# Hybrid S5 and RG-LRU layer: a scratch tensor laid out by channel and stored from ACT's queue, and loads moved from SP's queue to GpSimd's

## The chip, the core and the metric

The kernel runs on one core of one Trainium2 chip. A core has a matrix engine (TensorE, PE in the views; its weight load is PEld), a vector engine (VectorE, DVE), an activation engine (ScalarE, ACT), a general one (GpSimd, POOL), a sequencer for transfers (SyncE, SP) and 16 DMA engines. Each engine takes its own instructions in order and waits on semaphores for the others. SP, ACT and POOL can each issue DMAs; an issue is an instruction in that engine's order. The metric is the device time of one execution in microseconds.

## The reference

One layer over 2048 latent tokens (a 32 by 64 grid) behind 256 context tokens, model width 1024, all in float32. A projection of the normed input gives four parts of 1024 channels each: the S5 input, its gate, the RG-LRU input, its gate. Two recurrences run in both directions, and an output projection joins them:

```python
z = (rmsnorm(h, norm_g[layer]) * (1.0 + sc[:, None]) + sh[:, None]) @ w_in[layer]
u_s5, g_s5, u_lru, g_lru = jnp.split(z, cuts, axis=-1)
y_s5, _ = s5_branch(u_s5, *s5p, init=fin_s5, need_out=True)
y_lru, _ = rglru_branch(to_col_major(u_lru, rows), *lrup, init=fin_lru, need_out=True)
y_lru = to_row_major(y_lru, rows)
h_next = h + gt[:, None] * mix_out(y_s5, g_s5, y_lru, g_lru, w_out[layer])
```

The S5 branch is a complex diagonal recurrence in 64 groups of 16 channels. The RG-LRU branch is a short convolution, two sigmoid gates per direction from 64 by 64 block matrices (16 heads), and a gated scan. `mix_out` multiplies each result by the SiLU of its gate and projects 2048 channels to 1024.

## The kernel before

Every large product is made of three matmuls on numbers split into a high and a low part (`mm3`, lines 248 to 250). The weights of the input projection come in tiles of 128 columns, 512 KB each: `wload` (line 231) loads one into `wraw`, of which there are two, and ACT and DVE split it (lines 240 and 241). The projection runs in two halves of 1024 tokens, half 0 with the context; half 1 reloads the split weights as `w` from a DRAM scratch, WS (line 267).

The S5 input goes through a DRAM scratch, ZU. Before, ZU is laid out by half, step, channel in the group, group and chunk: `[2, T, 8, G, NCH]`. For each block of 128 channels ACT copies the context's part into a tile `zsc` (line 328) and the latent part, in two copies, into a tile `zst` (line 334). `zst` has a single buffer. SP stores each tile in two DMAs (lines 330 and 349), of 64 KB for zsc and 256 KB for zst. While half 0 does this, PE, DVE and ACT also build the S5 tables (W, Wt, psw, kk, lines 630 to 700).

The RG-LRU stage works on eight blocks of 128 channels, two heads each; "head b" below is block b. Its convolution result goes to the scratch XC (POOL's queue, line 383). For head b the loads are `gw` (gate weights, line 402), `xs` (the block with its two heads swapped, two DMAs of 576 KB, line 410) and `xc` (the block, 1152 KB, line 415), all with one buffer and all on SP's queue. `gates` multiplies (line 427) and takes the sigmoids (line 431); then follow tanh, exp and square root on ACT; `finish` runs the scans on DVE (lines 438 to 453) one head later, loads the output gate GL into the dead tile of rr (line 449, POOL's queue) and stores the result to the scratch YL (line 455, POOL's queue). `rr` has three buffers and `gi` four. In this stage PE's order is the one in the code, with the second half's projections between the gates; on all other engines, and in all other stages, a scheduler orders the instructions by priorities and modelled times.

After it the S5 stages run: `s5_inputs` reads ZU as `u` (two groups to a load, line 762), multiplies it by `wt`, and DVE scans the states chunk by chunk (lines 774 to 778); `s5_outputs` reads `u` again and multiplies by `mt` and `et`. As filler beside them `out_lru` multiplies y_lru by the output weights: it loads YL in 16 tiles with `wload` (SP's queue) and stores sums to the scratch HP (POOL's queue, line 864). The gated S5 result and the last product close the kernel.

Of the kernel before, what the change touches and what calls it, by code (L numbers as in the profile page):

```python
# [17 lines left out]
D = 1024  # L18
# [5 lines left out]
G = 64  # L24
NCH = 144
T = 16
# [20 lines left out]
class Block:  # L47
# [180 lines left out]
        return load  # L228


    def wload(self, src):

        raw = self.wp.tile([P, KT, P], F32, tag="wraw", bufs=2, name="wraw")
        self.nc.sync.dma_start(out=raw, in_=src)
        return raw

    def wsplit(self, raw, copy):
# [14 lines left out]
    def projections(self, half, kinds):  # L252

        nc = self.nc
# [38 lines left out]
        raw, nxt = self.first if half == 0 else (load(0), None)  # L293
        w = split(raw, 0)
        raw = nxt or load(1)
        for i, (kind, b, tiles) in enumerate(blocks):
            whi, wlo = w[:, 0], w[:, 1]
            r = slice(b * P, (b + 1) * P)
            if kind == "u_lru" and tiles[0] != 1:
                u = self.conv_input(half, b)  # L300
            if kind == "u_s5":
                st = self.stp.tile([P, T, 64], F32, tag="st4", bufs=1, name="zst")
            for tl in tiles:
                n = 256 if tl == "c" else 512
                xh, xl = self.xh[tl]
                ps = self.psM.tile([P, 512], F32, tag="mm", name="pp")
                for k in range(KT):
                    self.mm3(ps[:, :n], lambda k: whi[:, k, :], lambda k: wlo[:, k, :],
                             lambda k: xh[:, k, :n], lambda k: xl[:, k, :n], (k,))
                    if k < KT - 1:  # L310
                        yield
                if kind == "u_lru":
                    pos = 1 if tl == "c" else (3 if half else LC + 4) + tl % 2 * 512
                    nc.scalar.copy(out=u[:, pos:pos + n], in_=ps[:, :n])
                    if tl == "c":
                        self.conv(half, b, u, 0)
                elif kind == "g_lru":
                    o = self.stp.tile([P, 512], F32, tag="st2", bufs=2, name="ust")
                    if half:
                        nc.scalar.activation(out=o, in_=ps, func=AF.Sigmoid)  # L320
                        nc.vector.tensor_mul(out=o, in0=ps, in1=o)
                    else:
                        nc.scalar.activation(out=o, in_=ps, func=AF.Silu)
                    nc.scalar.dma_start(out=self.GL[r, tl * 512:tl * 512 + 512], in_=o)
                elif kind == "u_s5":
                    if tl == "c":
                        sc = self.stp.tile([P, T, 16], F32, tag="st2", bufs=2, name="zsc")
                        nc.scalar.copy(out=sc[:, ::-1, :], in_=ps[:, :256].rearrange("p (c j) -> p j c", j=T))
                        for kt in range(2):
                            nc.sync.dma_start(out=self.ZU[kt, :, :, b * 8:b * 8 + 8, 0:16].rearrange("h j g c -> g (h j) c"),  # L330
                                          in_=sc[:, kt * 8:kt * 8 + 8, :])
                    else:
                        o = (tl % 2) * 32
                        nc.scalar.copy(out=st[:, ::-1, o:o + 32], in_=ps.rearrange("p (j r) -> p j r", j=T))
                else:
                    o = self.stp.tile([P, 512], F32, tag="st2", bufs=2, name="gst")
                    nc.scalar.activation(out=o.rearrange("p (j a r) -> p a j r", j=8, a=2),
                                         in_=ps.rearrange("p (a j r) -> p a j r", a=2, j=8), func=AF.Silu)
                    nc.scalar.dma_start(out=self.GS[tl, r].rearrange("d j c -> d (j c)"), in_=o)
                if tl == tiles[0] and i + 1 < len(blocks):  # L340
                    w = split(raw, i + 1)
                    raw = load(i + 2)
                yield
            if kind == "u_lru" and tiles[-1] == both[-1]:
                self.conv(half, b, u)
            if kind == "u_s5":
                cs = slice(80, NCH) if half else slice(16, 80)
                for kt in range(2):
                    nc.sync.dma_start(out=self.ZU[kt, :, :, b * 8:b * 8 + 8, cs].rearrange("h j g c -> g (h j) c"),
                                      in_=st[:, kt * 8:kt * 8 + 8, :])  # L350


    def conv_input(self, half, b):
# [33 lines left out]
    def lru(self, lp, le):  # L387

        nc, v = self.nc, self.nc.vector
# [3 lines left out]
        rows = lambda b: slice(b * P, (b + 1) * P)  # L393
        big = lambda tag, n, pool=lp: pool.tile([P, N], F32, tag=tag, bufs=n, name=tag)

        def weights(b):

            gw = le.tile([P, 2, 2, 64], F32, tag="gw", bufs=1, name="gw")
            for w, name in enumerate(("lru_w_a", "lru_w_x")):
                for e in range(2):  # L400
                    src = self.io[name][0, :, 2 * b + e].rearrange("d i j -> i d j")
                    nc.sync.dma_start(out=gw[w * 64:w * 64 + 64, :, e, :], in_=src)
            return gw

        def load_xs(b):

            xs = big("xs", 1, le)
            for e in range(2):
                o = b * P + 64 - e * 64
                nc.sync.dma_start(out=xs[e * 64:e * 64 + 64, :], in_=self.XC[o:o + 64, :])  # L410
            return xs

        def load_xc(b):
            xc = big("xc", 1, le)
            nc.sync.dma_start(out=xc, in_=self.XC[rows(b), :])
            return xc

        def gates(b, d, gw, xcs, rr, gi):
# [39 lines left out]
        gw = weights(0)  # L458
        xs, xc = load_xs(0), load_xc(0)
        yield 4  # L460
        prev = iter(())
        for b in range(8):
# [9 lines left out]
            if b < 7:  # L472
                xs, gw, xc = load_xs(b + 1), weights(b + 1), load_xc(b + 1)
# [283 lines left out]
    def load_u(self, gp, g):  # L757

        u = gp.tile([P, 2, 2, NCH], F32, tag="u", bufs=3, name="u")
        for kt in range(2):  # L760
            src = self.ZU[kt, :, :, g:g + 2].rearrange("h j g c -> (h j) (g c)")
            self.nc.sync.dma_start(out=u[:, kt].rearrange("p g c -> p (g c)"), in_=src)
        return u

    def s5_scan(self, sp, zt, hb):
# [84 lines left out]
    def out_lru(self, wl, hr):  # L850

        nc = self.nc

        def load(j):
            src = self.YL.rearrange("(b p) t -> p b t", p=P)[:, :, j * P:(j + 1) * P]
            raw = self.wload(src)
            if j % 2:
                ht = self.stp.tile([P, T, 64], F32, tag="st4", bufs=1, name="hr1").rearrange("p a b -> p (a b)")
            else:
                ht = hr.tile([P, D], F32, tag="hr", bufs=1, name="hr0")  # L860
            return raw, ht
# [183 lines left out]
    def build(self):  # L1045
        tc, nc = self.tc, self.nc
        with ExitStack() as es:
# [4 lines left out]
            self.XC = dt("XC", [D, LC + L])  # L1052
            self.GL = dt("GL", [D, L])
            self.YL = dt("YL", [D, L])
            self.ZU = dt("ZU", [2, T, 8, G, NCH])
            self.GS = dt("GS", [4, D, T, 32])
            self.YT = dt("YT", [G, T, 8, 2, P])
            self.ZD = dt("ZD", [D, 8, 2, P])
# [165 lines left out]
```

## Time and profile before

| what | value |
|---|---|
| median of three runs | 1836.4 us (1836.33 to 1843.17) |
| profiled execution | 1834.38 us |
| its span | 1832.6 us |
| mean granted clock of PE | 0.969 |
| busy: PE, DVE, ACT, POOL | 1703.5, 1127.4, 864.0, 135.7 us |

The profile is of one execution. The rows further down come from six views. The *page* lists the busiest groups: line, engine, operation, output and inputs, count, then busy time and mean ns, then idle time ahead of them. The *chain* on the page follows the end of the program back to what released each step. A *windows* row is a stretch: its limits and length, busy time (and instructions) of PE, PEld, DVE, ACT and POOL, then the granted clock as a share of full speed, the mean busy share of the 16 DMA engines, and GB/s. A *waits* row names the engine and what it was about to do, what it waited for, the sum, the times and the longest. A *timeline* row is start, duration, engine (SPq is SP's issuing), line, operation, and in brackets the idle time before it and its releaser. A *tile* row gives min/median/max of a duration.

### The profile page before, as it was taken

The numbers are of one execution on the slowest core, as the hardware profiler recorded it, in microseconds if no ns is written. First come the engines' busy times: TensorE is split into PE (matmuls) and PEld (weight loads), VectorE is DVE, ScalarE is ACT, GpSimd is POOL, SyncE is SP. The second block draws the span as 40 slices with busy tenths as digits, with TensorE's granted clock in tenths as the row PEclk, the third lists the DMA queues.
The fourth block names the chain that finished last, engine by engine and source line by source line (L and its number), as shares of the span: only waits on it lengthen the run. The fifth ranks groups of instructions, "written<-read, shape, count | busy, mean of one in ns | idle before, by whom it ended". The sixth has DMA issues, their size and how long they took to land.

```text
span 1832.6 us, 26083 instructions
## 1 busy us (share of the span) xinstructions
PE 1703.5 (93%) x9785; PEld 1378.7 (75%) x9785; DVE 1127.4 (62%) x2006; ACT 864.0 (47%) x1376; POOL 135.7 (7%) x276
## 2 busy tenths in 40 slices
PE   7787899999998997989999899899999999999998
PEld 2666678888877664555567788778898899998886
DVE  5787788777354475679768049898600156336663
ACT  2622222222365386778675798525565443222221
POOL 1021111111110000000000000000000000001111
PEclk9898899999999998989999899999999999999999
DMA  8696577577654754566774988628898657557563
GB/s 258 157 219 182 170 209 230 190 258 270 223 182 151 242 155 165 172 209 206 202 203 133 293 280 263 200 90 263 268 284 263 194 169 211 144 156 219 187 195 89
DMA packets 315631, 373.56 MB, mean 204 GB/s; under 512 B 124669, under 2 KB 258417, under 8 KB 303218
## 3 DMA queue, kind: packets, MB, share of 16 engines
q1 hardware_dynamic: 267312, 235.04, 45.4%
q0 software_dynamic: 21824, 103.30, 15.1%
q10 hardware_dynamic: 26370, 33.57, 5.4%
q8 instruction: 77, 1.26, 0.3%
q14 instruction: 48, 0.39, 0.1%
HBM read 233.49 MB, written 138.35 MB: 203 GB/s over the span
## 4 chain that ended last, share of the span: by engine, by line
PE 55%; DMA 14%; DVE 12%; issue 9%; ACT 7%; SPq 2%; POOL 1%; ACTq 0%; DVEq 0%; POOLq 0%
PE pp L248 6%; PE pp L249 6%; PE pp L250 6%; PE po L250 5%; PE po L248 5%; PE po L249 5%; DMA ZU<-zst 4%; PE pgl L250 3%; PE pgl L248 3%; PE pgl L249 3%; PE py L811 2%; PE py L809 2%; DMA rr<-GL 2%; PE pg L427 2%; DVE p L774 2%
## 5 line engine op out<-in xcount | busy, mean ns | idle before, releaser
L248 PE MATMUL pp<-x,w 128*128 128x512 f32 x1024 | 420.4, 411 | 14.2 <-DMA w<-WS 12.3
L250 PE MATMUL pp<-x,w 128*128 128x512 f32 x1024 | 409.3, 400 | 4.7 <-DVE w L241 4.7
L249 PE MATMUL pp<-x,w 128*128 128x512 f32 x1024 | 409.4, 400 | 0.0
L248 PEld LDWEIGHTS pp<-x,w 128*128 128x128 f32 x1024 | 195.9, 191 | 91.0 <-issue 48.6
L250 PEld LDWEIGHTS pp<-x,w 128*128 128x128 f32 x1024 | 196.1, 191 | 48.9 <-DVE w L241 6.0
L249 PEld LDWEIGHTS pp<-x,w 128*128 128x128 f32 x1024 | 196.5, 192 | 39.9 <-issue 1.3
L241 DVE TENSOR_TENSOR w<-wraw,w 128x1024 fp32r<-128x1024 f32 x66 | 80.5, 1221 | 157.1 <-ACT w L240 143.2
L240 ACT CAST w<-wraw 128x1024 fp32r<-128x1024 f32 x66 | 69.4, 1051 | 159.8 <-PE pp L250 95.3
L381 DVE SCALAR_TENSOR_TENSOR xcv<-uc,vcol,xcv 128x256 f32<-128x256 f32 (+2 forms) x72 | 73.2, 1016 | 56.3 <-ACT xcv L378 54.5
L248 PE MATMUL po<-x,w 128*128 128x512 f32 x256 | 104.1, 407 | 0.8 <-ACT x L841 0.8
L249 PE MATMUL po<-x,w 128*128 128x512 f32 x256 | 100.7, 393 | 0.7 <-DVE x L842 0.7
L250 PE MATMUL po<-x,w 128*128 128x512 f32 x256 | 100.5, 392 | 0.0
L427 PE MATMUL pg<-xs,gw 64*64 64x512 f32 (+1 forms) x320 | 90.8, 594 | 10.3 <-ACT gi L431 10.3
L248 PE MATMUL po<-ws,yh 128*128 128x512 f32 x256 | 99.6, 389 | 0.0
L249 PE MATMUL po<-ws,yh 128*128 128x512 f32 x256 | 99.6, 389 | 0.0
L250 PE MATMUL po<-ws,yl 128*128 128x512 f32 x256 | 99.6, 389 | 0.0
L427 PE MATMUL pg<-xc,gw 64*64 64x512 f32 (+1 forms) x320 | 91.3, 594 | 8.1 <-ACT rr L431 5.3
L746 PE MATMUL pw<-u,wt 128*128 128x144 f32 x512 | 77.2, 300 | 13.3 <-DMA wt<-WD 10.3
L746 PEld LDWEIGHTS pw<-u,wt 128*128 128x128 f32 x512 | 73.0, 201 | 21.2 <-ACT z L753 11.5
L811 PE MATMUL py<-h,et 128*128 128x128 f32 x512 | 79.8, 280 | 9.8 <-ACT h L804 9.6
L774 DVE TENSOR_TENSOR p<-z,A 128x128 f32<-128x128 f32 x288 | 79.9, 291 | 6.3
L809 PE MATMUL py<-u,mt 128*128 128x128 f32 x512 | 79.4, 278 | 0.0
(259 smaller groups left out, 3518.9 us busy)
## 6 DMA issues: line engine op xcount, KB each, us to landing
wraw<-in_w_in_dram SPq DMA_DIRECT2D x50, 512.0 KB
WS<-w POOLq DMA_DIRECT2D x24, 1024.0 KB, 7.3
w<-WS SPq DMA_DIRECT2D x24, 1024.0 KB
u<-ZU SPq DMA_DIRECT2D x128, 144.0 KB
ED<-E POOLq DMA_DIRECT2D x16, 1024.0 KB, 6.1
WD<-Wt POOLq DMA_DIRECT2D x32, 512.0 KB, 5.1
wt<-WD SPq DMA_DIRECT2D x32, 512.0 KB
et<-ED SPq DMA_DIRECT2D x32, 512.0 KB
```

Source lines behind the costliest of these rows:

```text
L240: copy(out=w[:, 0], in_=raw)
L241: self.nc.vector.tensor_sub(out=w[:, 1], in0=raw, in1=w[:, 0])
L248: nc.tensor.matmul(ps, lhsT=whi(k), rhs=xhi(k), start=(k == 0), stop=False)
L249: nc.tensor.matmul(ps, lhsT=whi(k), rhs=xlo(k), start=False, stop=False)
L250: nc.tensor.matmul(ps, lhsT=wlo(k), rhs=xhi(k), start=False, stop=(k == KT - 1))
L381: nc.vector.scalar_tensor_tensor(out=xc, in0=u[:, o + k:o + k + N], scalar=cw[:, k * 8 + b:k * 8 + b + 1], in1=xc, op0=ALU.mult, op1=ALU.add)
L427: nc.tensor.matmul(pss[w][e * 64:e * 64 + 64, :n], lhsT=gw[ws, d, e, :], rhs=xcs[(w + e) % 2][ws, o:o + n], start=True, stop=True, tile_po ...
L746: nc.tensor.matmul(pw[:, c, :], lhsT=w[:, gi, kt, c, :], rhs=u[:, kt, :], start=(kt == 0), stop=(kt == 1))
L774: v.tensor_mul(out=p, in0=cur.unsqueeze(1).to_broadcast([P, 2, 2, 32]), in1=self.A16[:, :, :, gs])
L809: nc.tensor.matmul(o, lhsT=ms(m[:, i * 8:i * 8 + T]), rhs=u[:, i, 16:], start=(i == 0), stop=False)
L811: nc.tensor.matmul(o, lhsT=ms(e[:, i, gi]), rhs=h[:, i, :], start=False, stop=(i == 1))
```

## The change

Three things. ZU is laid out by half, channel, step in the group's eight and chunk, `[2, D, 8, NCH]`; its stores are issued by ACT, and the loads of `u` read two pieces of 576 bytes per partition where they read one of 1152. The loads gw, xs and xc are issued by POOL. The y_lru tiles of `out_lru` are loaded by POOL's queue, for which `wload` takes an engine.

```diff
-    def wload(self, src):
+    def wload(self, src, eng=None):
 
         raw = self.wp.tile([P, KT, P], F32, tag="wraw", bufs=2, name="wraw")
-        self.nc.sync.dma_start(out=raw, in_=src)
+        (eng or self.nc.sync).dma_start(out=raw, in_=src)
...
                         for kt in range(2):
-                            nc.sync.dma_start(out=self.ZU[kt, :, :, b * 8:b * 8 + 8, 0:16].rearrange("h j g c -> g (h j) c"),
-                                          in_=sc[:, kt * 8:kt * 8 + 8, :])
+                            nc.scalar.dma_start(out=self.ZU[kt, r, :, 0:16], in_=sc[:, kt * 8:kt * 8 + 8, :])
...
                 for kt in range(2):
-                    nc.sync.dma_start(out=self.ZU[kt, :, :, b * 8:b * 8 + 8, cs].rearrange("h j g c -> g (h j) c"),
-                                      in_=st[:, kt * 8:kt * 8 + 8, :])
+                    nc.scalar.dma_start(out=self.ZU[kt, r, :, cs], in_=st[:, kt * 8:kt * 8 + 8, :])
...
                     src = self.io[name][0, :, 2 * b + e].rearrange("d i j -> i d j")
-                    nc.sync.dma_start(out=gw[w * 64:w * 64 + 64, :, e, :], in_=src)
+                    nc.gpsimd.dma_start(out=gw[w * 64:w * 64 + 64, :, e, :], in_=src)
...
                 o = b * P + 64 - e * 64
-                nc.sync.dma_start(out=xs[e * 64:e * 64 + 64, :], in_=self.XC[o:o + 64, :])
+                nc.gpsimd.dma_start(out=xs[e * 64:e * 64 + 64, :], in_=self.XC[o:o + 64, :])
...
             xc = big("xc", 1, le)
-            nc.sync.dma_start(out=xc, in_=self.XC[rows(b), :])
+            nc.gpsimd.dma_start(out=xc, in_=self.XC[rows(b), :])
...
         for kt in range(2):
-            src = self.ZU[kt, :, :, g:g + 2].rearrange("h j g c -> (h j) (g c)")
-            self.nc.sync.dma_start(out=u[:, kt].rearrange("p g c -> p (g c)"), in_=src)
+            src = self.ZU[kt, g * 16:(g + 2) * 16].rearrange("(g h) j c -> (h j) g c", g=2)
+            self.nc.sync.dma_start(out=u[:, kt], in_=src)
...
             src = self.YL.rearrange("(b p) t -> p b t", p=P)[:, :, j * P:(j + 1) * P]
-            raw = self.wload(src)
+            raw = self.wload(src, nc.gpsimd)
...
-            self.ZU = dt("ZU", [2, T, 8, G, NCH])
+            self.ZU = dt("ZU", [2, D, 8, NCH])
```

The order of PE's instructions is the same but for one group that moves one place. On ACT the stores of ZU enter. This is ACT in half 0, at blocks 1 and 2 of the S5 input (L334 and L333 copy into zst, L328 into zsc), before:

```order
L334 COPY zst<-pp 128x16x32
L328 COPY zsc<-pp 128x16x16
L686 COPY kk<-psk 128x240
L687 COPY kk<-psk 128x240
L334 COPY zst<-pp 128x16x32
L240 CAST w<-wraw 128x1024
L665 COPY Wt<-psw 128x512 x2
L334 COPY zst<-pp 128x16x32
L328 COPY zsc<-pp 128x16x16
```

and now:

```order
L333 COPY zst<-pp 128x16x32
L348 DMA ZU<-zst 1024x1x64 x2
L328 COPY zsc<-pp 128x16x16
L684 COPY kk<-psk 128x240
L330 DMA ZU<-zsc 1024x1x16 x2
L685 COPY kk<-psk 128x240
L333 COPY zst<-pp 128x16x32
L240 CAST w<-wraw 128x1024
L663 COPY Wt<-psw 128x512 x2
L333 COPY zst<-pp 128x16x32
L348 DMA ZU<-zst 1024x1x64 x2
```

The issues now stand between the copies of the block and those of the tables.

On SP, in the RG-LRU stage at head 5 and the start of half 1's S5 input, the loads of w stood between the loads of xs, gw and xc and the stores of zst:

```order
L410 DMA xs<-XC 64x2304
L267 DMA w<-WS 128x2048
L410 DMA xs<-XC 64x2304
L402 DMA gw<-in_lru_w_a_dram 64x2x64 x2
L402 DMA gw<-in_lru_w_x_dram 64x2x64 x2
L415 DMA xc<-XC 128x2304
L267 DMA w<-WS 128x2048
L1179 DMA gt<-GT 128x1024
L267 DMA w<-WS 128x2048
L349 DMA ZU<-zst 8x128x64 x2
```

Now SP goes from one load of w to the next, and on to the weights of the last projection and the loads of u:

```order
L267 DMA w<-WS 128x2048 x14
L1177 DMA gt<-GT 128x1024
L267 DMA w<-WS 128x2048 x6
L234 DMA wraw<-in_w_in_dram 128x8x128 x6
L760 DMA u<-ZU 128x2x144 x2
L739 DMA wt<-WD 128x1024
```

Nothing is left on SP in this stage that waits for anything but a buffer of w.

On POOL the order there, from head 2's GL to the XC store of block 7, was before:

```order
L449 DMA rr<-GL 128x2048
L455 DMA YL<-gi 128x2048
L383 DMA XC<-xcv 128x1026
L363 MEMSET uc 128x2
L449 DMA rr<-GL 128x2048
L455 DMA YL<-gi 128x2048
L383 DMA XC<-xcv 128x1026
```

and is now, from head 3's GL to the first loads of head 6:

```order
L447 DMA rr<-GL 128x2048
L453 DMA YL<-gi 128x2048
L408 DMA xs<-XC 64x2304 x2
L400 DMA gw<-in_lru_w_a_dram 64x2x64 x2
L400 DMA gw<-in_lru_w_x_dram 64x2x64 x2
L413 DMA xc<-XC 128x2304
L381 DMA XC<-xcv 128x1026
L447 DMA rr<-GL 128x2048
L453 DMA YL<-gi 128x2048
L408 DMA xs<-XC 64x2304 x2
```

The loads of head 5 come behind GL and YL of head 3, those of head 6 behind head 4's, those of head 7 behind head 5's. The loads of heads 3 and 4 stand between GL and YL of heads 1 and 2.

## Rows read from the trace of the kernel before

**Rows 1.** The page: the chain by engine, and the costliest group of matmuls.
```profile
PE 55%; DMA 14%; DVE 12%; issue 9%; ACT 7%; SPq 2%; POOL 1%; ACTq 0%; DVEq 0%; POOLq 0%
...
L248 PE MATMUL pp<-x,w 128*128 128x512 f32 x1024 | 420.4, 411 | 14.2 <-DMA w<-WS 12.3
```

**Rows 2.** Windows by stage (columns as told above), and the first 25 us.
```profile
125.00:225.00 100.00, 78.46 (x455) 61.70 (x454) 74.04 (x95) 19.85 (x38) 16.81 (x27) 0.86 0.61 171
225.00:500.00 275.00, 273.22 (x1663) 221.24 (x1662) 197.65 (x258) 80.02 (x142) 46.84 (x92) 1.00 0.70 230
...
625.00:1000.00 375.00, 341.06 (x1680) 221.80 (x1679) 267.70 (x131) 268.80 (x299) 11.85 (x26) 0.96 0.58 177
...
1078.00:1228.00 150.00, 141.28 (x723) 120.11 (x721) 138.62 (x594) 88.48 (x182) 2.67 (x5) 0.98 0.61 198
1228.00:1650.00 422.00, 413.94 (x3051) 392.34 (x3052) 186.76 (x503) 189.34 (x307) 5.86 (x11) 0.99 0.71 215
...
125.00:150.00 25.00, 21.04 (x111) 17.20 (x117) 23.76 (x31) 4.54 (x8) 7.04 (x8) 0.93 0.62 164
```

**Rows 3.** Waits of ACT and of SP's queue.
```profile
ACT zst L334 <- DMA ZU<-zst: 100.7, 12, 16.3
...
SPq L410 <- PE pg L427: 118.0, 7, 34.5
SPq L415 <- DVE gi L471: 46.7, 5, 17.5
```

**Rows 4.** Timeline of ACT, half 0: a copy into zst.
```profile
158.96 0.59 ACT L334 COPY zst<-pp 128x512 f32<-128x512 f32 x1 [11.66 <-DMA ZU<-zst]
```

**Rows 5.** Timeline of PE behind that copy.
```profile
160.73 1.11 PE L662 MATMUL psw<-ident,W 128*128 128x128 f32 x4 [4.87 <-DVE W L632]
...
162.06 0.63 PE L249 MATMUL pp<-x,w 128*128 128x512 f32 x1
```

**Rows 6.** Windows of shorter stretches.
```profile
125.00:127.00 2.00, 2.00 (x10) 1.62 (x9) 2.00 (x2) 0.00 (x0) 0.53 (x1) 1.00 0.41 68
700.00:725.00 25.00, 13.12 (x61) 8.52 (x61) 11.42 (x8) 24.76 (x23) 0.38 (x2) 0.79 0.53 208
775.00:800.00 25.00, 20.20 (x87) 9.30 (x84) 23.28 (x11) 13.88 (x21) 1.56 (x4) 0.80 0.42 134
846.50:858.50 12.00, 11.14 (x49) 8.71 (x47) 11.86 (x8) 9.93 (x9) 1.07 (x2) 1.00 1.00 343
861.00:985.00 124.00, 116.88 (x591) 76.43 (x589) 91.32 (x39) 90.67 (x100) 3.23 (x6) 0.99 0.65 181
1020.00:1078.00 58.00, 53.75 (x335) 47.53 (x334) 2.45 (x2) 54.02 (x129) 0.00 (x0) 0.96 0.91 290
```

**Rows 7.** The tile ZU: issue times of its stores, min/median/max in ns.
```profile
L349 SPq DMA_DIRECT2D ZU<-zst x32: 583/1206/7050, 124.1 to 983.5; - x32
L330 SPq DMA_DIRECT2D ZU<-zsc x16: 1078/4944/8694, 108.8 to 270.4; - x16
```

**Rows 8.** The chain of waits from 683 to 770 us: start, length, what.
```profile
684.48 11.44 DMA rr<-GL
...
744.61 12.03 DMA rr<-GL
```

**Rows 9.** DMA issues: KB each and median us to landing.
```profile
rr<-GL POOLq DMA_DIRECT2D x8, 1024.0 KB, 7.5
YL<-gi POOLq DMA_DIRECT2D x8, 1024.0 KB, 4.8
```

**Rows 10.** Timeline of ACT behind the first of those loads.
```profile
699.53 0.19 ACT L364 COPY uc<-halo 128x3 f32<-128x3 f32 x1 [15.16 <-DVE xcv L381]
```

**Rows 11.** Timelines of POOL, SP and PE before the gates of head 5.
```profile
846.54 0.53 POOL L455 DMA_DIRECT2D YL<-gi  x1 [10.08 <-DVE gi L453]
...
848.75 0.33 SPq L415 DMA_DIRECT2D xc<-XC  x1
...
858.60 0.43 PE L427 MATMUL pg<-xc,gw 64*64 64x256 f32 x1
```

## The prediction

> **What bounds the kernel now.** I read the chain that ended last first: more than half of it is PE, and the three other large shares, DMA, DVE and ACT, are places where PE waits or runs behind somebody [rows 1]. The table by stages then says where PE has room [rows 2]. It is full in the stretch from 225 to 500 us (273.22 of 275) and nearly so from 1228 to 1650 (413.94 of 422), so nothing that a transfer does there can show. It has room in two stretches that the change touches. From 125 to 225 us, where half 0 of the S5 input is projected, PE works 78.46 of 100 us at a granted clock of 0.86; from 625 to 1000, the RG-LRU stage, 341.06 of 375. From 1078 to 1228 PE has room too, but DVE is busy for 138.62 of the 150 us with the serial scan of the two S5 states: whatever a transfer saves there goes to DVE's next step.
>
> The list of waits names who holds the first stretch up: ACT waited 100.7 us, 12 times, before the copy into zst, for the stores of the zst before [rows 3]. zst has one buffer, so the copy of block b cannot start until both stores of block b-1 have landed. One of them is in the timeline of ACT, 11.66 us before 158.96 [rows 4]. ACT takes its instructions in order, so the copies of kk and Wt behind that zst wait too, DVE's W behind them, and PE: 4.87 us of idle before 160.73, and after it matmuls of 0.63 us [rows 5], against the 0.411 us of the page's mean for line 248 [rows 1]. The clock thus takes a second toll: where PE had been idle the granted level is 1.2 of 2.4 GHz for some microseconds.
>
> Why the stores are slow is in the windows: while almost nothing but pieces of ZU moves, the DMA engines' share stays at 0.41, although with other traffic it reaches 1.00 [rows 6]. I read this as a store that is dealt to half of the 16 engines: its outer dimension is 8 (8x128x64 in the order of SP). SP pays for it as well. An issue for zst takes 1206 ns at the median and up to 7050, one for zsc 4944 and up to 8694 [rows 7], and the weight loads stand behind them.
>
> In the RG-LRU stage the chain of waits shows rr<-GL twice with 11.44 and 12.03 us from issue to landing [rows 8], against a median of 7.5 [rows 9]. The xs loads were issued at the same moment on another queue and moved with it. After the first of these ACT had been idle for 15.16 us [rows 10], and then had so much to catch up that PE worked only 13.12 us between 700 and 725; 775 to 800 has 20.20 at a clock of 0.80 [rows 6]. SP itself stood 118.0 us before xs and 46.7 before xc [rows 3], with the loads of w behind them.
>
> **The change part by part.**
>
> *ZU's layout and its queue, half 0.* The same 1024 pieces per store go to an outer dimension of 1024, so I expect all 16 engines, and landing in about half the time. An ACT wait of 11.66 us ends with a landing that came that much too late [rows 4]; the stores of a block were then under way for more than 12 us. In half the time they land some 6 us sooner or more, and the issues no longer stand behind SP's other ones: I take the wait as gone, or 3 us long at most. The room in this stretch is 100 - 78.46 = 21.5 us of idle PE, and I estimate 4 us for the clock: after each of three such gaps some 4 us of matmuls run at 0.63 instead of 0.411 us, a third of that lost. 25.5 in all. Not all of it comes back. In the first 25 us DVE is busy for 23.76 and PE idle for 4 [rows 2]: that is DVE's own limit, and stays. And ACT now issues: four issues to a block, each at least the 583 ns of the fastest zst issue and, at the median, 1206 [rows 7], so 2.3 to 4.8 us a block in which ACT can't copy. ACT is busy for only 19.85 of the 100 us, so I charge one microsecond of each block, 4.5 in all. 25.5 - 4 - 4.5 = **17 us**. The bounds: 0, if the issues on ACT stretch as they did on SP, and 25.
>
> *ZU in half 1.* From 861 to 985 PE is busy for 116.88 of 124 us [rows 6]: at most 7 us, against 16 issues that enter an ACT with much to do (268.80 of 375 in the stage). Taken as plus 3 and minus 3: nothing.
>
> *xs, xc and gw on POOL's queue.* What it takes away is SP's standing (118.0 and 46.7 us): the w loads behind go out when their buffer is free. What it does to the path is that xs now stands behind rr<-GL on one queue, so GL need not share the engines with it. GL lands in 11.44 and 12.03 us now and should take 6 to 7.5: 4 to 6 us earlier twice, less at the other heads. The idle PE of the stage is 375 - 341.06 = 34 us; 11.9 of it lies in 700 to 725, 4.8 in 775 to 800, where the clock costs more. I take **12 us**: twice 5, and 2 of clock. Bounds: 25 (all but a quarter of the idle time), and the loss priced below. POOL pays some 56 issues of about 0.55 us (that of 846.54 is 0.53) and is busy for 11.85 of the 375 us: nothing by itself; its order is another matter.
>
> *The y_lru loads on POOL's queue.* Sixteen issues leave SP, where they stood before loads of the S5 outputs. From 1078 to 1228 DVE sets the pace, and behind it PE idles only 8 us in 422 [rows 2]: I take 2 us, between 0 and 4. They share POOL's order with the stores of HP, which ACT's copies wait for only through a single buffer; DVE's scan hides that.
>
> *u loads with two pieces per partition.* 128 loads have pieces of 576 instead of 1152 bytes. Between 1020 and 1078 the engines' share is 0.91, but ACT is busy there for 54.02 of 58 us [rows 6], so ACT hides most of it. I charge 1 us, between 0 and 4.
>
> The sum is made on the profiled execution: 1834.4 - 17 - 12 - 2 + 1 = 1804.4. Its time is 2 us below the median of the three runs, 1836.4; I predict **1804**.
>
> **The rivals.**
>
> *ACT pays for the issues.* On SP the ZU issues stretched to 5 and 8 us since the queue was full. If they stretch alike on ACT, the copies of Wt and kk stand behind them as they stood behind the wait: 17 goes to about 0, and in half 1 some of the 12 is eaten. 1834 - 2 + 1, between 1826 and 1838. For it: the pieces stay as small and as many, and the row on SP doesn't show whether they or the load of SP's queue made the issues long. Against it: the fastest zst issue had the same pieces and took 583 ns [rows 7], so the pieces alone don't make it long, and the engines that take them double.
>
> *Only the first stretch gains.* In the RG-LRU stage DMA engines are at 1.00 from 846.5 to 858.5 with 343 GB/s [rows 6]: where bytes are the limit another queue brings nothing, and ACT and PE have nearly equal work. Then 12 goes: 1834.4 - 17 + 1 - 2 = 1816.
>
> The Trainium skill has a rule against the change on the same page, section "Issuing engines are not separate DMA queues": transfers from any issuing engine run on the same 16 DMA engines, and another issuer saves only the sequencer's time. By it the xs, xc, gw and y_lru moves are worth only SP's standing; the row of 343 GB/s agrees for that stretch. It is this rival, 1816.
>
> *POOL's order makes it slower.* In the new order xs, gw and xc of head 5 stand behind YL of head 3, on a queue that is served in order. YL was issued at 846.54, xc of head 5 at 848.75, the gates of that head began at 858.60 [rows 11]. Now YL, xs and xc, 1024 + 1152 + 1152 = 3328 KB, must pass in the 12 us from 846.54. At 343 GB/s they need 10 and are just in time. At the pace of a lone rr<-GL, 1024 KB in 7.5 us [rows 9], they need 24, and the gates start 12 us late. Three heads have this order (5, 6, 7): 36 us, and the 12 us are not won: 1834.4 - 17 - 2 + 1 + 36 = 1852. It decides from the point where POOL's queue moves less than about 280 GB/s. For it: the median of YL is 1024 KB in 4.8 us [rows 9], 213 GB/s. Against it: one transfer alone pays its own latency, and queued ones overlap.
>
> *The gain is larger.* The idle time of both stretches goes almost wholly, 25 + 25 us: 1785 or a little below.
>
> **How the numbers follow.** Forecast, 1793 to 1812: 0.42. Only the first stretch, 1812 to 1825: 0.21. Larger gain, 1776 to 1793: 0.11. ACT pays, 1826 to 1838: 0.13. POOL's order, above 1840: 0.13. I take half a per cent, 9 us, as what a measurement of this kernel tells from no change: faster means below about 1826. Faster 0.42 + 0.21 + 0.11 = 0.74; same 0.13; slower 0.13. The range from 1782 to 1838 leaves out POOL's order and a third of the larger gain, 0.17 in all. The likeliest case's own range is 1793 to 1812.
>
> **What would show each step.** ZU right: ACT's wait before zst nearly gone from the list of waits, PE busy above 90% there, the clock near 1.0, the stage done some 17 us earlier; issues for ZU near 0.6 us on ACT's queue. If they are 3 us and more, ACT paid. GL right: rr<-GL on the chain with 5 to 8 us and no ACT idle of 15 us before the second head. POOL's order: the gates' matmuls (line 427 now) wait for xs or xc, or POOL idles long before YL with xs behind it. SP's list must have lost the waits before xs and xc either way. Wrong altogether would be a stage from 1078 on that moves by more than 5 us: then the y_lru or the u loads do what I priced at nothing.

## The result

| kernel | median of its runs | against before |
|---|---|---|
| before | 1837.8 us (4 runs) | 1 |
| changed | 1816.3 us (1811.1 to 1820.2, 4 runs) | 0.9876 [0.9843, 0.9909] |
| changed, in a later series | 1816.0 us (6 runs; before 1832.9) | 0.9899 [0.9876, 0.9923] |

The change makes the kernel faster by 1.0 to 1.2 per cent, some 17 to 21 us; the prediction said 1804, with 1782 to 1838 as its range. 1816 lies outside the likeliest case's own range, 1793 to 1812, and in that of the rival "Only the first stretch gains", 1812 to 1825, and the gain is short of the 30 us that were forecast. The span of the profiled execution fell from 1832.6 to 1813.2 us.

The page of the changed kernel, busy time by engine: PE is busy for 5 us less with the same instructions, which I put down to the clock; POOL has 72 more instructions, the moved issues.

```profile
PE 1698.5 (94%) x9785; PEld 1372.1 (76%) x9785; DVE 1128.0 (62%) x2006; ACT 864.2 (48%) x1376; POOL 181.8 (10%) x348
```

PE runs the same 9785 instructions in both kernels, in the same order but for one group. So a stretch of one trace can be matched to the stretch of the other that holds the same instructions. The windows of the changed kernel that answer to 125 to 225, to 600 to 625, to 625 to 1000 and to 1228 to 1650 us of before are these (columns: limits, length, busy and count of PE, PEld, DVE, ACT, POOL, clock, DMA share, GB/s); the counts of PE, 455, 110, 1680 and 3051, show the match:

```profile
126.30:203.70 77.40, 71.02 (x455) 55.05 (x454) 71.47 (x93) 20.51 (x39) 16.14 (x26) 1.00 0.71 216
577.70:612.30 34.60, 27.51 (x110) 21.86 (x109) 12.98 (x13) 3.72 (x6) 2.24 (x5) 0.90 0.78 244
612.30:979.30 367.00, 338.48 (x1680) 221.86 (x1679) 268.45 (x131) 268.39 (x299) 39.56 (x75) 0.96 0.57 179
...
1207.30:1630.70 423.40, 414.61 (x3051) 392.72 (x3052) 185.53 (x493) 188.32 (x305) 12.41 (x18) 0.99 0.72 214
```

and the second of them in the kernel before:

```profile
600.20:625.20 25.00, 25.00 (x110) 20.31 (x109) 12.63 (x12) 3.82 (x6) 0.65 (x2) 1.00 1.00 319
```

Against [rows 2] the first stretch went from 100 to 77.4 us, PE's idle time from 21.5 to 6.4 and the clock from 0.86 to 1.00: 22.6 us won. The second went from 25 to 34.6: 9.6 us lost, in a place that the prediction did not look at. The RG-LRU stage went from 375 to 367: 8 won. From 1228 on 1.4 were lost. Together that is -22.6 + 9.6 - 8 + 1.4 = -19.6, and the spans differ by 19.4. So the total is what one of the rivals said, 1816, though not for its reason.

The wait for the stores shrank, though it did not go. From the waits of the whole changed kernel, to be held against [rows 3]:

```profile
ACT zst L333 <- DMA ZU<-zst: 30.7, 6, 10.6
```

The tile ZU, issue times in ns, min/median/max, against [rows 7]:

```profile
L348 ACTq DMA_DIRECT2D ZU<-zst x32: 520/521/1687, 120.3 to 962.2; - x32
L330 ACTq DMA_DIRECT2D ZU<-zsc x16: 520/1265/4033, 102.6 to 236.6; - x16
```

And from ACT's timeline the longest issue of this stretch with the wait behind it, and the other wait that is left there:

```profile
146.27 4.65 ACTq L330 DMA_DIRECT2D ZU<-zsc  x2
153.60 0.59 ACT L333 COPY zst<-pp 128x512 f32<-128x512 f32 x1 [7.37 <-DMA ZU<-zst]
...
187.49 0.58 ACT L333 COPY zst<-pp 128x512 f32<-128x512 f32 x1 [6.35 <-DMA ZU<-zst]
```

100.7 us of waiting became 30.7, 12 times became 6; in the first stretch alone 50.8 us in 4 waits became 13.7 in 2. The bracket counts ACT's own issuing as idle time: of the 7.37 us 4.65 are the issue in the line above, and the copy starts 2.7 us after it. While ZU alone moves, the DMA share is now twice that of [rows 6], in a window of the changed kernel:

```profile
122.00:124.00 2.00, 1.25 (x22) 0.64 (x21) 2.00 (x3) 0.00 (x0) 0.00 (x0) 1.00 0.85 163
```

(The share adds up the times of packets, which overlap on an engine, so it can pass 1.)

What is late next in this stretch is DVE: 71.47 of 77.40 us busy.

At the start of the RG-LRU stage PE waits 7.09 us for a w. From POOL's timeline of the changed kernel:

```profile
580.32 1.03 POOL L408 DMA_DIRECT2D xs<-XC  x2 [2.94 <-DMA XC<-xcv]
581.34 0.57 POOL L413 DMA_DIRECT2D xc<-XC  x1
```

From SP's, the w in question:

```profile
580.75 0.32 SPq L267 DMA_DIRECT2D w<-WS  x1
```

And from PE's, the wait and the matmul after it:

```profile
598.35 0.77 PE L248 MATMUL pp<-x,w 128*128 128x512 f32 x1 [7.09 <-DMA w<-WS]
598.91 0.63 PE L249 MATMUL pp<-x,w 128*128 128x512 f32 x1
```

That w, 1024 KB, took 17.6 us to come. In the same microseconds POOL sent for xs and xc of head 0, 2304 KB that are wanted only at the first gates, and from 582 to 600 us the engines' share was 1.04 at 304 GB/s. They were as busy in this stretch before (1.00 at 319 GB/s), but one queue held w, then xs, then another w, then xc, and w passed first. From SP's timeline of the kernel before:

```profile
602.91 0.40 SPq L267 DMA_DIRECT2D w<-WS  x1
...
609.65 1.74 SPq L410 DMA_DIRECT2D xs<-XC  x2
613.79 0.33 SPq L267 DMA_DIRECT2D w<-WS  x1
614.16 0.43 SPq L415 DMA_DIRECT2D xc<-XC  x1
```

After the wait the matmuls take 0.63 us, so the 7.09 us became 9.6.

Inside the stage rr<-GL lands sooner, as forecast: 5.1 us at the median and 7.7 at most, where [rows 8, 9] had 12.03 and 7.5. From the tile GL of the changed kernel:

```profile
DMA to landing us min/median/max: 5.0/5.1/7.7
```

ACT's idle time before the second head [rows 10] shrank, but did not go:

```profile
681.58 0.19 ACT L362 COPY uc<-halo 128x3 f32<-128x3 f32 x1 [10.24 <-DVE xcv L379]
```

What PE waited for there is another load. Before, its longest idle time in the stage was a wait for a w, which SP issued right behind xc:

```profile
705.75 0.33 SPq L415 DMA_DIRECT2D xc<-XC  x1
706.18 0.85 SPq L267 DMA_DIRECT2D w<-WS  x2
...
713.55 0.77 PE L248 MATMUL pp<-x,w 128*128 128x512 f32 x1 [9.90 <-DMA w<-WS]
```

In the changed kernel that wait is gone, and PE waits for xc instead:

```profile
701.25 0.66 PE L425 MATMUL pg<-xc,gw 64*64 64x256 f32 x1 [6.77 <-DMA xc<-XC]
```

From 700 to 733 us of before's time this gives 4.6 to 4.9 us in each of the eight kernels that move the loads of heads 1 to 4. The five that leave them on SP lose 0.4 to 2.4 us there.

### The profile page after: what moved, and what is told of

The parts are those of the page before. It is cut to its first block, busy times and chain, and to the rows that moved or that the text cites. A ratio compares the mean times of both kernels' runs of the same rounds, so it can differ in the third digit from the quotient of the medians.

```text
span 1813.2 us, 26054 instructions
## 1 busy us (share of the span) xinstructions
PE 1698.5 (94%) x9785; PEld 1372.1 (76%) x9785; DVE 1128.0 (62%) x2006; ACT 864.2 (48%) x1376; POOL 181.8 (10%) x348
## 5 line engine op out<-in xcount | busy, mean ns | idle before, releaser
L809 PE MATMUL py<-h,et 128*128 128x128 f32 x512 | 80.7, 282 | 10.8 <-ACT h L802 10.7
```

What stands on the lines that cost most here:

```text
L809: nc.tensor.matmul(o, lhsT=ms(e[:, i, gi]), rhs=h[:, i, :], start=False, stop=(i == 1))
```

## The experiments

I give for each kernel its edit, what was expected, what was measured, and what follows. "PE's lead" is by how much the n-th PE instruction starts earlier than the same one in the profiled execution of before, at the instruction that stood there at the named time. The table shows how the lead changes from stage to stage (minus is won, plus is lost; times are those of before).

| kernel | ZU | xs, xc, gw on POOL | to 225 | 225-600 | 600-625 | 625-850 | 850-1000 | 1000-1229 | 1229-1800 |
|---|---|---|---|---|---|---|---|---|---|
| changed | new, ACT | heads 0-7 | -21.4 | -1.1 | +9.6 | -10.5 | +2.6 | -1.6 | +2.8 |
| e12 (the same again) | new, ACT | heads 0-7 | -22.6 | -1.3 | +9.7 | -10.6 | +6.7 | -1.5 | +4.2 |
| e1 | new, ACT | none | -18.7 | +1.2 | 0.0 | -2.1 | -1.8 | -0.8 | +6.3 |
| e2 | old, SP | heads 0-7 | -7.3 | -0.4 | +10.6 | -10.9 | +14.0 | -0.1 | -0.4 |
| e3 | new, ACT | heads 0-7 | -19.1 | +1.6 | +8.4 | -10.9 | +7.9 | -0.4 | +1.4 |
| e4 | new, ACT | heads 1-7 | -20.9 | 0.0 | 0.0 | -10.7 | +2.8 | -1.2 | +0.7 |
| e5 | new, SP | none | -27.2 | +1.3 | 0.0 | +0.4 | -9.1 | -0.2 | +1.7 |
| e6 | old, ACT | none | +8.9 | +20.0 | 0.0 | -0.9 | +16.1 | -1.3 | -0.2 |
| e8 | new, ACT | heads 1-4 | -21.4 | -1.5 | 0.0 | -11.3 | +0.5 | -1.6 | +4.1 |
| e9 | old, SP | none | -6.0 | 0.0 | 0.0 | +0.3 | +2.3 | -1.0 | +0.7 |
| e10 | new, SP | heads 1-4 | -25.1 | -0.7 | 0.0 | -11.8 | +0.4 | +2.0 | -0.7 |
| e11 | new, SP | heads 0-7 | -26.9 | -0.7 | +5.7 | -12.0 | +6.2 | -0.3 | +4.0 |
| e13 | new with spare rows, SP | none | -4.0 | -0.5 | 0.0 | 0.0 | +3.2 | +1.6 | +3.7 |

Each line is one execution. The first column of e2, e9 and e13 shows how far one can be trusted there: their stores are as slow as those of before, and they still lead by 4 to 7 us at 225, so the profiled execution of before was slow in this stretch by about that much. In the later columns, too, a few us are within what one execution tells: the profiled executions of e1 and e3 were the slowest of their four, 8 and 12 us above their medians.

**e1: ZU alone.** The changed kernel with two parts taken back:

```diff
-            raw = self.wload(src, nc.gpsimd)
+            raw = self.wload(src)
-                    nc.gpsimd.dma_start(out=gw[w * 64:w * 64 + 64, :, e, :], in_=src)
+                    nc.sync.dma_start(out=gw[w * 64:w * 64 + 64, :, e, :], in_=src)
...
```

(xs and xc likewise.)

> The kernel before with ZU's new layout and its stores on ACT's queue alone; the loads of the RG-LRU heads and of y_lru stay on SP's queue. Theory A (the stores landing sooner are the whole gain; in the changed kernel the loads moved to GpSimd cost 9.6 us at the start of the RG-LRU stage, since xs and xc of head 0 pass the w that PE needs, and give about 8 us back inside it): PE is 22 us ahead of the kernel before at 225 us of its time, and still 21 to 23 ahead at 625 and at 1000, since nothing else is moved: some 21 us faster in all, the same as the changed kernel within 4 us. Theory B (the loss at the start of the RG-LRU stage comes from ZU or from half 0 being early, and the moved loads only give): 22 ahead at 225, 13 at 625, 13 at 1000: 12 us faster in all.

Measured: 1809.9 us, ratio 0.9874 [0.9840, 0.9908], the same as the whole change. PE led by 18.7 us at 225 and by 17.5 at 625: nothing is lost at the start of the stage. Theory A.

**e2: the loads of the heads alone**, the mirror of e1 on the kernel before.

> The kernel before with gw, xs and xc of all heads on GpSimd's queue alone. Theory A: PE waits some 7 us for w at the start of the RG-LRU stage, 8 to 10 us lost by 625 us; inside the stage some 8 us come back since GL lands sooner and SP no longer holds w back: within 3 us of the kernel before. Theory B (the moved loads only give): 6 to 10 us faster, with no loss at 625.

Measured: 1840.2 us against 1834.9, ratio 1.0030 [1.0012, 1.0048]: slower by 5 us, a little more than theory A had it. PE waited for w at the start of the stage, by the waits of PE from 590 to 630 us:

```profile
PE pp L248 <- DMA w<-WS: 9.0, 1, 9.0
```

10.9 us came back up to 850, and 14.0 were lost behind it: 6.6 at the gates of head 5, and most of the rest at one wait of 8.20 us for ACT, in this one execution. That the moved loads only give is wrong.

**e3: y_lru back on SP**, one line of the changed kernel:

```diff
-            raw = self.wload(src, nc.gpsimd)
+            raw = self.wload(src)
```

> The changed kernel with the y_lru tiles back on SP's queue. PE lost 3 to 4 us between 1078 and 1400 us in the changed kernel. If the y_lru loads on GpSimd's queue did that: this kernel is 3 us faster than the changed one, some 24 us faster than before. If the u loads of two pieces did it: no difference to the changed kernel, some 21 us faster than before. If y_lru was worth the 2 us that the prediction gave it: 19 us faster than before.

Measured: 1811.3 us, ratio 0.9868 [0.9840, 0.9895], against the changed kernel's 0.9876 and 0.9899 in two series. Not to be told apart from it: y_lru's queue is worth 0, give or take some 8 us. Whether the 2 us of the prediction are in that stays open.

**e4: head 0 alone back on SP**, in the changed kernel, for gw, xs and xc:

```diff
-            nc.gpsimd.dma_start(out=xc, in_=self.XC[rows(b), :])
+            (nc.gpsimd if b else nc.sync).dma_start(out=xc, in_=self.XC[rows(b), :])
```

> The changed kernel with gw, xs and xc of head 0 alone back on SP's queue, behind the w that is needed first; heads 1 to 7 stay on GpSimd's. Theory A: the 7 us wait for w and the slow clock after it go, PE is 22 us ahead of the kernel before at 625 us, and the kernel is 8 to 10 us faster than the changed one, some 30 us faster than before. Theory B (the loss there has another cause, or is made up elsewhere in the stage anyway): the same as the changed kernel, some 21 us faster than before.

Measured: 1807.6 us, ratio 0.9864 [0.9836, 0.9892]; its profiled span was 1803.7. The total overlaps with that of the changed kernel, so the eight us are not proved by it, but the stage is plain. The window of e4 that holds 109 of the same 110 PE instructions:

```profile
579.40:604.30 24.90, 24.90 (x109) 20.26 (x108) 12.75 (x12) 3.81 (x6) 0.65 (x2) 1.00 1.00 331
```

and SP's timeline in e4, with w first again:

```profile
582.12 0.42 SPq L267 DMA_DIRECT2D w<-WS  x1
...
588.85 1.89 SPq L408 DMA_DIRECT2D xs<-XC  x2
592.95 0.33 SPq L267 DMA_DIRECT2D w<-WS  x1
593.33 0.43 SPq L413 DMA_DIRECT2D xc<-XC  x1
```

PE is busy through all 24.9 us. In the table all five kernels with head 0 on POOL lose 5.7 to 10.6 us there, and all others 0.0.

**e5: the layout, from SP's queue.** ZU's new layout alone, on the kernel before:

```diff
-                    nc.sync.dma_start(out=self.ZU[kt, :, :, b * 8:b * 8 + 8, cs].rearrange("h j g c -> g (h j) c"),
-                                      in_=st[:, kt * 8:kt * 8 + 8, :])
+                    nc.sync.dma_start(out=self.ZU[kt, r, :, cs], in_=st[:, kt * 8:kt * 8 + 8, :])
```

(zsc, the shape of ZU and the loads of u as in the change.)

> The kernel before with ZU's new layout, but its stores still issued by SP; nothing else is moved. Theory A1 (the gain of half 0 comes from the stores being dealt to 16 engines): PE is 15 to 20 us ahead of the kernel before at 225 us, issues for zst shrink from 1206 ns to below 700 at the median, and the kernel is 15 to 20 us faster. Theory A2 (it comes from leaving SP's queue, where the weight loads and the stores stand behind each other): below 8 us.

Measured: 1802.3 us against 1832.7, ratio 0.9821 [0.9794, 0.9847]: 30 us faster, more than the whole change, and more than theory A1 had expected. The tile ZU in e5:

```profile
L348 SPq DMA_DIRECT2D ZU<-zst x32: 512/614/3830, 118.7 to 948.3; - x32
L330 SPq DMA_DIRECT2D ZU<-zsc x16: 513/1637/4197, 105.0 to 232.6; - x16
```

The window of the same 455 PE instructions in e5, and one in which ZU moves alone:

```profile
123.40:198.00 74.60, 71.01 (x455) 55.07 (x454) 69.73 (x91) 20.25 (x38) 16.14 (x26) 1.00 0.75 222
...
120.00:122.00 2.00, 2.00 (x8) 1.71 (x8) 2.00 (x3) 0.90 (x3) 0.30 (x1) 0.50 1.04 213
```

SP's own issues shrank to a half and a third at the median [rows 7]. The layout is the gain; leaving SP's queue isn't needed for it.

**e6: the old layout, from ACT's queue**, the other half of ZU's part:

```diff
-                    nc.sync.dma_start(out=self.ZU[kt, :, :, b * 8:b * 8 + 8, cs].rearrange("h j g c -> g (h j) c"),
+                    nc.scalar.dma_start(out=self.ZU[kt, :, :, b * 8:b * 8 + 8, cs].rearrange("h j g c -> g (h j) c"),
```

> The kernel before with its old layout of ZU, the stores issued by ACT; nothing else is moved. Theory A1: the stores still land slowly, ACT's wait before zst stays near 10 us a block, and the issues of zsc, 4944 ns at the median on SP, now stop ACT: between 5 us faster and 10 us slower than before. Theory A2: 15 us faster or more.

Measured: 1878.5 us, ratio 1.0248 [1.0208, 1.0287], 46 us slower; theory A1 had bounded the harm at 10. Only the issuing queue differs from the kernel before, so this is what issuing from ACT costs with slow stores. ACT's timeline shows such an issue: two issues of zsc take 14.11 us, and the next copy starts when they are through.

```profile
177.58 14.11 ACTq L330 DMA_DIRECT2D ZU<-zsc  x2
191.81 0.59 ACT L334 COPY zst<-pp 128x512 f32<-128x512 f32 x1 [14.26 <-DMA ZU<-zst]
```

The store of zst had not landed much sooner: its pieces passed from 176.2 to 190.7 us, so this copy alone doesn't tell the issue from the landing; the 46 us do. This is the rival "ACT pays for the issues" in full; it needs slow stores, and the new layout takes most of it away.

**e13: the new layout, its rows not mergeable.** As e5, with a spare row after every 16 channels:

```diff
-            self.ZU = dt("ZU", [2, D, 8, NCH])
+            self.ZU = dt("ZU", [2, G, 129, NCH])
...
-                    nc.sync.dma_start(out=self.ZU[kt, r, :, cs], in_=st[:, kt * 8:kt * 8 + 8, :])
+                    nc.sync.dma_start(out=self.ZU[kt, b * 8:b * 8 + 8, 0:128, cs], in_=st[:, kt * 8:kt * 8 + 8, :])
```

> As the kernel with the new layout on SP's queue alone, but with one unused row of 576 bytes after every group of 16 channels in ZU. The pieces, their sizes and their places are the same but for that; the rows of a block can no longer be taken as one dimension of 1024, so the order shows the stores as 8x128x64 again, as before. If the outer dimension of 8 is what kept the stores on half of the engines: the DMA share returns to 0.4 to 0.5 while ZU alone moves, the issues of zsc to 4 to 5 us, and the kernel is within 8 us of the kernel before. If where the pieces lie in memory made the stores fast: 28 to 32 us faster than before, as with the layout alone.

Measured: 1834.2 us, ratio 0.9990 [0.9978, 1.0001]: the whole 30 us are gone. The pieces lie where they lay in e5 but for the spare rows, and the store is 8x128x64 again. The tile ZU in e13:

```profile
L348 SPq DMA_DIRECT2D ZU<-zst x32: 583/1218/9243, 122.6 to 982.0; - x32
L330 SPq DMA_DIRECT2D ZU<-zsc x16: 817/4778/8850, 106.9 to 264.5; - x16
```

and a window in which ZU alone moves:

```profile
136.00:138.00 2.00, 2.00 (x6) 1.61 (x6) 2.00 (x5) 0.00 (x0) 0.00 (x0) 0.50 0.42 37
```

The share is back at 0.42 and the issues at their old length. So the outer dimension decides, and not the place of the pieces. The Trainium skill, page "DMA: Bandwidth & Descriptors", section "Why a DMA increments its semaphore by 16 and not by 1", gives the rule: a DMA is dealt to the largest number of engines, up to 16, that divides the slowest dimension of both sides, here 8 and 16. The shares, 0.41 and 0.42 with 8 and 0.85 to 1.04 with 1024, agree.

The profiles also hold a count. The row of DMA queue 10, which grows where ACT issues the stores (packets, MB, share), for the kernel before, e6 (8, from ACT) and e1 (1024, from ACT):

```profile
q10 hardware_dynamic: 26370, 33.57, 5.4%
...
q10 hardware_dynamic: 75906, 43.00, 8.6%
...
q10 hardware_dynamic: 76290, 43.01, 8.4%
```

The 48 stores of ZU have 1024 pieces each, 49152 in all. e6 has 49536 packets more than before and e1 49920: beyond its pieces that is 8 packets for each store with an outer dimension of 8, and 16 with 1024. They are 4 bytes long; I read them as one closing write of each engine that took part. On SP's queue e13 and e5 differ by the same 384.

**e8: heads 1 to 4 alone on POOL.** The changed kernel with head 0, heads 5 to 7 and y_lru back on SP:

```diff
-            nc.gpsimd.dma_start(out=xc, in_=self.XC[rows(b), :])
+            (nc.gpsimd if 1 <= b <= 4 else nc.sync).dma_start(out=xc, in_=self.XC[rows(b), :])
```

> The changed kernel with gw, xs and xc on GpSimd's queue for heads 1 to 4 only, and on SP's for head 0 and for heads 5 to 7, and y_lru on SP's queue. Theory A (head 0's loads pass the w that PE needs; for heads 5 to 7 GpSimd's order puts them behind YL, and PE lost 5 us before head 5; for heads 1 to 4 they give 9 us): 22 ahead of the kernel before at 625 us, 30 at 800, no 3.4 us wait before the gates of head 5, some 30 us faster than before, 5 to 10 faster than the changed kernel. If the moved loads are worth nothing even there: 21 to 25 us faster than before, as with ZU alone.

Measured: 1796.3 us against 1832.7, ratio 0.9799 [0.9773, 0.9825]: 36 us faster. Up to 625 the lead was 22.9, at 850 34.2, and the loss before head 5 is gone. From 625 to 850 us the eight kernels that move the loads of heads 1 to 4 win 10 to 12 us; e1, which doesn't, wins 2.1.

What heads 5 to 7 lose shows at head 5 of the changed kernel, as the prediction's third rival described it [rows 11]. POOL's timeline has YL first, then xs, then xc:

```profile
821.40 0.53 POOL L453 DMA_DIRECT2D YL<-gi  x1 [7.22 <-DVE gi L451]
821.93 1.03 POOL L408 DMA_DIRECT2D xs<-XC  x2
...
825.28 0.59 POOL L413 DMA_DIRECT2D xc<-XC  x1
```

and on PE's timeline the gates begin late:

```profile
838.59 0.56 PE L425 MATMUL pg<-xc,gw 64*64 64x256 f32 x1 [3.43 <-issue]
```

The profile names no releaser here, but by its packets the last piece of xc landed at 837.6 us, 12.3 after its issue, and the pieces of xs and xc, 2304 KB, moved only from 825.7 on, when nearly all of YL had passed. From 853 to 865 us of before's time the six kernels with head 5 on POOL (the changed one, e2, e3, e4, e11, e12) lose 5.2 to 6.6 us, and the others 0.0 to 1.2.

**e9: the pieces of u alone.** On the kernel before, both sides of each load with the two groups in reverse:

```diff
-            src = self.ZU[kt, :, :, g:g + 2].rearrange("h j g c -> (h j) (g c)")
-            self.nc.sync.dma_start(out=u[:, kt].rearrange("p g c -> p (g c)"), in_=src)
+            src = self.ZU[kt, :, :, g:g + 2].rearrange("h j g c -> (h j) g c")[:, ::-1, :]
+            self.nc.sync.dma_start(out=u[:, kt, ::-1, :], in_=src)
```

> The kernel before with nothing changed but that each load of u reads its two groups as two pieces of 576 bytes, in the other order of groups, instead of one of 1152; the data that arrive are the same. The prediction charged 1 us, between 0 and 4. If the 1 to 6 us that the changed kernels lost between 1228 and 1400 us come from these pieces: 2 to 5 us slower than before, with et arriving later than py needs it. If not: within 1 us of before.

Measured: 1834.8 against 1832.7, ratio 1.0009 [0.9990, 1.0029]: between 2 us faster and 5 slower. The eleven kernels with two pieces lose 2.6 us on average after 1229 in the table, the two others with one piece win 0.3. That is no proof, but it lies within the 0 to 4 that the prediction gave.

**e10, e11, e12: on one chip.** e10 is e8 with the stores of ZU on SP's queue, e11 the changed kernel with them on SP's queue, e12 the changed kernel again. The edit of e10 and e11 beside e8 and the change:

```diff
-                    nc.scalar.dma_start(out=self.ZU[kt, r, :, cs], in_=st[:, kt * 8:kt * 8 + 8, :])
+                    nc.sync.dma_start(out=self.ZU[kt, r, :, cs], in_=st[:, kt * 8:kt * 8 + 8, :])
```

> ZU's new layout with its stores on SP's queue, gw, xs and xc on GpSimd's queue for heads 1 to 4 only, y_lru on SP's queue. If the two gains add: 26 us ahead of the kernel before at 625 us (layout), 35 at 800 (heads 1 to 4), 43 at 1000 (half 1 without ACT's issues): 38 to 43 us faster than before, below 1795. If SP's waits come back with the stores, so that heads 1 to 4 bring nothing here: 30 us faster, as with the layout alone.

> The changed kernel with the stores of ZU issued by SP, all else as in the change. Theory A (issuing on ACT costs 5 us in half 0 and 5 in half 1, and the loads of head 0 on GpSimd's queue still cost 9.6): 5 to 10 us faster than the changed kernel, which is run beside it. If issuing on ACT costs nothing: the same.

> The changed kernel itself once more, beside the two others, so that they are compared on one chip: 18 to 24 us faster than before.

Measured: e10 1797.7 us (0.9800 [0.9775, 0.9825]), e11 1813.3 (0.9882 [0.9858, 0.9907]), e12 1816.0 (0.9899 [0.9876, 0.9923]); before 1832.9. e10 and e8 are the fastest kernels here, some 18 us below the change, and equal. Issuing from SP wins some 5 us more up to 225 than from ACT (25.1 to 27.2 against 18.7 to 22.6). In total that is not seen: e10 was 35 us faster and missed the 38 that adding both gains would give. One place is in its timelines: with xs and xc on SP again, the w for head 6 stood behind xc and came late.

```profile
854.71 0.33 SPq L413 DMA_DIRECT2D xc<-XC  x1
855.13 0.49 SPq L267 DMA_DIRECT2D w<-WS  x1
...
864.00 0.77 PE L248 MATMUL pp<-x,w 128*128 128x512 f32 x1 [6.29 <-DMA w<-WS]
```

e5 has the same loads and stores on SP and no such wait at this head, so this is a reading and not shown. The expectation for e11, 5 to 10 us, was missed too: 2.7 us between medians, with overlapping intervals. e12, expected to be 18 to 24 us faster, was 16.9 by the medians, just short of it.

## Why the prediction was right, and where it was not

*What bounds the kernel.* Right for the gains: they came in the two stretches named, 125 to 225 and the RG-LRU stage, and from 225 to 600 nothing moved (1.1 us). Wrong for the loss: 9.6 us went from 600 to 625, where no part of the forecast looked.

*ZU in half 0: predicted 17, measured 21.4 and 22.6* against the profiled execution of before. The mechanism was the one given, and e5, e6 and e13 show it: the outer dimension of 8. Against that one execution two terms were too small. PE's busy time fell by 78.46 - 71.02 = 7.4 us, where I had put 4 for the clock; and of the idle 21.5 us 15.1 went, where 21.5 - 4 - 4.5 = 13 was reckoned. The 4.5 for ACT's issues was right in size: SP's queue does some 5 us better. Part of the excess is the profile of before, slow here by the 4 to 7 us that e2, e9 and e13 lead; against those three the changed kernel wins 14 to 19. So 17 was about right, and whether the two terms were too small stays open. The wait before zst was to be gone, or 3 us long at most: two are left, of 7.37 and 6.35 us, and of these 2.7 and 3.1 lie behind ACT's own issues.

*ZU in half 1: predicted 0.* e1 won 1.8 there. From SP's queue it was 9.1 (e5), a little over the 7 us that I had bounded it by. That ACT's issues take this back is not shown: most of the difference is one wait for a w in e1, 4.97 us long, and e8 and e10, which differ in the same way, have 0.5 and 0.4.

*xs, xc and gw: predicted 12 won, measured 1.7 lost* (9.6 - 10.5 + 2.6), and alone, in e2, 5 us slower. This is the step that failed. The gain came near in size, 10.5 us from 625 to 850, but not by the sum that gave the 12: that counted GL landing 5 us sooner twice. GL did land sooner, yet PE's idle time from 700 to 725 us, which the prediction put down to ACT catching up, ended with a w that stood behind xc on SP's queue. It is this wait, 9.90 us, that went, and one of 6.77 for xc that came. GL's landing does stand ahead of the work on ACT and DVE that freed the buffer of xc, and no run parts the two causes; so the near size is in part luck. The loss was looked for in one place, behind YL at heads 5 to 7, and priced at 36 us or nothing; it was 5.3 at head 5, where one head was priced at 12, and from 850 to 1000 it came to 2.6 and 6.7 in two executions of the change, and up to 14.0 in e2. The larger loss, 9.6 us, lay before the stage, where the table of stages has no idle PE: from 600 to 625 PE was busy 25.00 of 25 us, with the DMA engines at a share of 1.00, a row that the prediction doesn't have. PE was full there only since SP's single queue let w pass before xs and xc. I had counted the release of w from behind xs as a gain, and not the other direction, xs released from behind w.

*y_lru 2, u pieces -1:* within what the runs can tell, neither shown.

*The rivals.* "Only the first stretch gains" hit the total, 1816, for a wrong reason: the moved loads were not worth nothing, they gave 10.5 and took 9.6 and 2.6. The Trainium skill's rule that stood beside that rival, section "Issuing engines are not separate DMA queues" of "DMA: Bandwidth & Descriptors", is borne out by the start of the stage: the loads of two queues shared the same engines, and w took 17.6 us. "ACT pays" is real with slow stores (e6) and costs some 5 us in half 0 with quick ones. "POOL's order" is real at head 5: e8 and e10, without it, lose 0.0 and 1.0 there against 5.3. The pace it gives for YL, 1024 KB in 4.8 us, is 218 GB/s and not 213, which changes nothing.

## What to carry to other kernels

Look at the shape of a store before its queue: an outer dimension of 8 kept 256 KB on half of the engines, and making its rows one dimension of 1024 was worth 30 us, more than all the moves of queues together. A queue is also an order: moving a load away frees what stood behind it, but lets the load itself pass what stood before it, so read the stretches without a wait, too, if the transfer engines are full there. And a move that gives in one loop round may cost in another; put the rounds that gain on the new queue and leave the others.

## What was not expected of the hardware

An issue can hold its engine for many microseconds. Two issues of zsc, 64 KB each in pieces of 64 bytes, held ACT for 14.11 us with an outer dimension of 8 (e6); with 1024 the median issue of zsc was 1.3 to 1.7 us, the fastest 0.51, and the longest 4.7. In those 14.11 us, up to 190.7, the pieces of the zst store ahead on the same queue were still passing, so the issue seems to have waited for them. From SP's queue as from ACT's, the long issues came with the outer dimension of 8, and the pieces were as small and as many in both.
